# A streaming encoder step on one core: five norms as one product each with a constant matrix, and a first stage loaded by single tiles

## The chip, the core and the metric

The kernel runs on one core of a Trainium2 chip. A core has a matrix engine (TensorE, "PE" in the profile, with its weight loads as "PEld"), a vector engine ("DVE"), a scalar engine ("ACT"), a general engine (GpSimd, "POOL") and a sequencer for transfers (SyncE, "SP"; "SPq" are the transfers that it issues). Each engine works off its own list of instructions in order and waits at semaphores. Matmuls read SBUF and write PSUM. The metric is the device time of one execution in microseconds (us), lower is better; the time of a kernel is the median of several runs.

## What is computed

One layer of a streaming encoder over 320 columns of tokens (256 of a prompt, 64 of a running stream), width 2048. The projection feeds an attention part and a gated part; both are normalised, joined and projected, and a squared-ReLU MLP follows.

```python
def rmsnorm(x, g):
    y = x * lax.rsqrt(jnp.mean(x * x, axis=-1, keepdims=True) + EPS)
    return y * g

z = rmsnorm(x, ln_g) @ w_in                      # 2048 -> 1024 q, 128 k, 128 v, 2048 gated
q, k = rmsnorm(q, q_g), rmsnorm(k, k_g)          # per head of 64
attn = sink_attention(q, k, v, bias, sinks)      # windows of 64-column chunks, 16 heads, 2 kv heads
u, v = gelu(zs)[..., :1024], rmsnorm(gelu(zs)[..., 1024:], g)
sgu = u * (W_s @ v + b_s)
mix = concat(rmsnorm(attn, g_a), rmsnorm(sgu, g_s))
x = x + mix @ w_out
x = x + square(relu(rmsnorm(x, ln_ffn) @ w_up)) @ w_down
```

The changed norms are those of `x` at the start ("rx" in the kernel), of `k` per head ("rk"), of the attention's output ("rm0", after the change "rm_a"), of the gated part's output ("rm1", "rm_s") and of `x` before the MLP ("r2").

## The kernel before

**Layout.** Activations lie transposed: a tile holds 128 rows of a feature dimension and 320 columns of tokens. `xT` has 16 such row tiles. A norm's factor is one number for each token, so it is needed as a 128x320 tile in which every row is the same; it is multiplied in behind the matmuls, when PSUM is read.

**Products.** `products` (L106) works through a weight matrix in chunks of four row tiles by 256 columns. For each chunk it loads `w_raw` (512 KB) on SP's queue; ACT rounds it to `w_hi` (L125), DVE takes the rest `w_lo` (L126), three buffers of each; PE then does `w_hi` times the high part, `w_hi` times the low part and `w_lo` times the high part of the activations (L136), 24 matmuls of 320 columns in a chunk, 96 in a product over 16 row tiles. All products accumulate in two PSUM buffers named `acc`, so that a third one begins only when DVE has read the first.

**First stage.** The first call (L196) makes two products at once: k and v (`kv_ps`, an `acc` buffer) and the first 256 columns of q (`q0_ps`). It also loads `xT` and splits it into `XH` (ACT, L178) and `XL` (DVE, L179). The first four row tiles are loaded one by one and converted in the written order (`keep_in_program_order`), the other twelve in chunks of four.

**The relative bias.** PE makes the bias row (L224), DVE copies it to `b_row` (L226), POOL's queue writes it to device memory as `b_dram` (L228), and 16 transfers of 48 KB read it back into `bias` (L236). These wait in the list `between`, and `load` (L94) puts four of them behind each of the next four weight loads, on the same SP queue. That queue is worked off in order, and the first of them waits until `b_dram` has landed; the weight load that stands behind four bias transfers is issued after them. So the second chunk of the product that follows the first stage (q's second 256 columns, "q1" below) is loaded only when the bias row has made its way.

**Norms.** The squares of `x` are summed on ACT and DVE (`ssq`), those of later norms by `add_square` (L377, ACT and POOL). `rstd_rows` (L154) multiplies the sums by a column of 1/n (three matmuls with one output column, in f32, which the trace shows as six), adds eps on DVE and takes the power -1/2 on POOL: the factors then lie on 128 partitions by 3. `spread` (L165) brings them back along the tokens with three matmuls against the identity, again six in the trace, and a DVE copy. For k (two heads) the same is done with `hsel`, `rkx` and L283.

**Order.** The tile framework's scheduler sets each engine's order from its own timeline, except where `issue_after` or `keep_in_program_order` bind it. x's squares are bound behind step 9 of the first stage (L242), and so is the bias product (L223). What follows q1 in PE's list are the products for q's columns 512 to 1024, four for the gated v with the attention between them, four for u, sixteen of 48 matmuls for `w_out`, and the MLP's 64 products.

Of the kernel before, what the change touches and what calls it, by code (L numbers as in the profile page):

```python
# [29 lines left out]
def hymba_step_kernel(ctx: ExitStack, tc: tile.TileContext, i, o):  # L30
# [55 lines left out]
    hsel = const.tile([P, 2], F32, name="hsel")  # L86
    nc.vector.memset(hsel, 0.0)
    nc.vector.memset(hsel[0:HD, 0:1], 1.0 / HD)
    nc.vector.memset(hsel[HD:P, 1:2], 1.0 / HD)
# [11 lines left out]
    def chunks(n, first):  # L101
        if first:
            return [(a, 1) for a in range(4)] + [(a, 4) for a in range(4, n, 4)]
        return [(a, 4) for a in range(0, n, 4)]

    def products(w, k0, nk, jobs, rh, rl, first=None, deep=None):  # L106
# [4 lines left out]
        for a, n in chunks(nk, first is not None):  # L111
# [4 lines left out]
            for j, (c0, ps) in enumerate(jobs):  # L116
# [7 lines left out]
                pin = tc.keep_in_program_order if first is not None and a < 4 else lambda ins: ins  # L124
# [29 lines left out]
    def rstd_rows(sq, weight, eps, h=1):  # L154

        st = misc()
        for t in range(3):
            nc.tensor.matmul(out=st[:, t * h:t * h + h], lhsT=sq[:, t * P:(t + 1) * P], rhs=weight, start=True, stop=True)  # L158
        r = sm.tile([P, 3 * h], F32, name="r_rows", tag="r_rows")
        nc.vector.tensor_scalar(out=r, in0=st[:, 0:3 * h], scalar1=eps, scalar2=None, op0=ALU.add)  # L160
        rs = sm.tile([P, 3 * h], F32, name="rs_rows", tag="rs_rows")
        nc.gpsimd.tensor_tensor(out=rs, in0=r, in1=nhalf[:, 0:3 * h], op=ALU.pow)
        return rs

    def spread(rs, name):  # L165

        bc = misc()
        for t, (t0, n) in enumerate(TT):
            nc.tensor.matmul(out=bc[:, t0:t0 + n], lhsT=rs[:, t:t + 1].to_broadcast([P, P]),  # L169
                             rhs=ident[:, 0:n], start=True, stop=True)  # L170
        out = sm.tile([P, T], F32, name=name, tag="rstd_b", bufs=2)
        nc.vector.tensor_copy(out=out, in_=bc[:, 0:T])
        return out

# [48 lines left out]
    with tc.issue_after(steps[9][2]):  # L223
        nc.tensor.matmul(out=b_ps[0:16, 0:255], lhsT=tab, rhs=oneh, start=True, stop=True)  # L224
# [27 lines left out]
    zk = sm.tile([P, T], F32, name="zk", tag="w2", bufs=4)
    nc.vector.tensor_tensor(out=zk, in0=kv_ps[:, 0, 0:T], in1=rx, op=ALU.mult)
    nc.vector.tensor_tensor(out=vT, in0=kv_ps[:, 1, 0:T], in1=rx, op=ALU.mult)
    sq = sums("ksq")
    nc.scalar.activation(out=sq[:, 0:T], in_=zk, func=AF.Square)
    rk = rstd_rows(sq, hsel, EPS, 2)
# [3 lines left out]
    def queries(g, q_ps):  # L261
# [8 lines left out]
        for b in range(5):  # L270
# [10 lines left out]
    bc = misc()  # L281
    for t, (t0, n) in enumerate(TT):
        nc.tensor.matmul(out=bc[:, t0:t0 + n], lhsT=rkx[:, t], rhs=ident[:, 0:n], start=True, stop=True)  # L283
    for dst, c in ((kn[:, 0:256], slice(0, 256)), (kn[:, 384:448], slice(256, 320))):
        nc.vector.scalar_tensor_tensor(out=dst, in0=zk[:, c], scalar=g_k, in1=bc[:, c], op0=ALU.mult, op1=ALU.mult)
# [17 lines left out]
    for g in range(1, 4):  # L303
        queries(g, product(w_in, 0, KT, g * 256, xh, xl))
# [98 lines left out]
    acc_v = sums("acc_v")  # L403
# [32 lines left out]
    for g in range(4):  # L436
# [24 lines left out]
    for half, (hi, lo, acc) in enumerate(((AH, AL, acc_a), (SH, SL, acc_s))):  # L461
        rm = spread(rstd_rows(acc, inv_1k, EPS), f"rm{half}")
        for g in range(8):
# [9 lines left out]
    r2 = spread(rstd_rows(acc_x, inv_dm, EPS), "r2")  # L473
# [94 lines left out]
```

## Time and profile before

| | |
|---|---|
| median of 3 runs | 1260.79 us (1259.16 to 1262.47) |
| the profiled execution: device time / span of the instructions | 1262.67 us / 1260.9 us |
| instructions in the trace | 20260 |
| DVE busy | 635.5 us (50% of the span) |
| ACT busy | 488.9 us (39%) |
| POOL busy | 104.1 us (8%) |
| moved by DMA | 187.79 MB, 149 GB/s in the mean |
| mean granted TensorE clock | 0.997 |

The page of a profile gives for each engine the time in which it had an instruction at work. The prediction takes its durations from this one execution. Its device time is 1.8 us over its span (what lies before the first and behind the last instruction), and 1.9 us over the median of the runs.

### The profile page before, as it was taken

How to read it: one execution, taken by the hardware profiler on the slowest of the kernel's cores; microseconds unless marked ns; L12 is line 12 of the kernel's file. 1: busy time of each engine (PE TensorE's matmuls, PEld its weight loads, DVE VectorE, ACT ScalarE, POOL GpSimd, SP SyncE). 2: the span in 40 equal slices, each digit the busy share in tenths (PEclk: the TensorE clock that was granted, in tenths of full speed). 3: DMA queues.
4: the chain of work that ended last, by engine and by line, in shares of the span. 5: the costliest groups of instructions: out<-in, count | busy, mean ns of one | idle time of the engine just before them, and what ended most of it. 6: DMA issues, size and time to landing. Idle time of an engine off the chain costs nothing.

```text
span 1260.9 us, 20260 instructions
## 1 busy us (share of the span) xinstructions
PE 1251.8 (99%) x8559; PEld 1238.0 (98%) x8559; DVE 635.5 (50%) x731; ACT 488.9 (39%) x636; POOL 104.1 (8%) x100
## 2 busy tenths in 40 slices
PE   8999999999999999999999999999999999999998
PEld 7998899999999999999999999999999999999998
DVE  6547857756864444444444444344444334444443
ACT  7335546523543342233333333344333333343221
POOL 1213443400310000000000000000000000000000
PEclk8999999999999999999999999999999999999999
DMA  9553334644445544445544444555444444544550
GB/s 281 168 141 106 97 115 125 213 142 147 148 143 150 151 149 150 150 149 151 151 150 151 151 150 151 151 150 150 151 150 150 145 149 149 150 152 160 170 168 32
DMA packets 186427, 187.79 MB, mean 149 GB/s; under 512 B 6464, under 2 KB 185856, under 8 KB 186336
## 3 DMA queue, kind: packets, MB, share of 16 engines
q1 hardware_dynamic: 185696, 185.43, 47.5%
q0 software_dynamic: 496, 1.03, 0.4%
q8 instruction: 67, 1.10, 0.4%
q14 instruction: 24, 0.20, 0.0%
q10 hardware_dynamic: 144, 0.03, 0.0%
HBM read 182.91 MB, written 3.32 MB: 148 GB/s over the span
## 4 chain that ended last, share of the span: by engine, by line
PE 98%; DMA 1%; SPq 0%; ACT 0%; POOL 0%; issue 0%; DVE 0%; POOLq 0%
PE acc L136 93%; PE misc L136 1%; PE q_ps L136 1%; DMA xT<-in_xT 1%; PE misc L365 1%; PE misc L371 1%; PE s_ps L327 1%; SPq L99 0%; PE misc L271 0%; PE misc L427 0%; PE misc L158 0%; POOL s L355 0%; PE misc L419 0%; PE misc L169 0%; PE misc L428 0%
## 5 line engine op out<-in xcount | busy, mean ns | idle before, releaser
L126 DVE TENSOR_TENSOR w_lo<-w_raw,w_hi 128x1024 fp32r<-128x1024 f32 x332 | 413.0, 1244 | 458.8 <-ACT w_hi L125 449.8
L125 ACT ACTIVATE w_hi<-w_raw 128x1024 fp32r<-128x1024 f32 x332 | 351.8, 1060 | 714.2 <-PE acc L136 675.7
L136 PE MATMUL acc<-H2H,w_hi 128*128 128x320 f32 x1024 | 316.6, 309 | 0.0
L136 PE MATMUL acc<-H2L,w_hi 128*128 128x320 f32 x1024 | 316.4, 309 | 0.0
L136 PE MATMUL acc<-H2H,w_lo 128*128 128x320 f32 x1024 | 316.4, 309 | 0.0
L136 PE MATMUL acc<-FH,w_hi 128*128 128x320 f32 x992 | 306.5, 309 | 0.0
L136 PE MATMUL acc<-FL,w_hi 128*128 128x320 f32 x992 | 306.5, 309 | 0.0
L136 PE MATMUL acc<-FH,w_lo 128*128 128x320 f32 x992 | 306.5, 309 | 0.0
L136 PEld LDWEIGHTS acc<-H2L,w_hi 128*128 128x128 f32 x1024 | 192.2, 188 | 0.0
L136 PEld LDWEIGHTS acc<-H2H,w_hi 128*128 128x128 f32 x1024 | 192.2, 188 | 0.0
L136 PEld LDWEIGHTS acc<-H2H,w_lo 128*128 128x128 f32 x1024 | 192.2, 188 | 0.0
L136 PEld LDWEIGHTS acc<-FH,w_hi 128*128 128x128 f32 x992 | 186.2, 188 | 0.0
L136 PEld LDWEIGHTS acc<-FL,w_hi 128*128 128x128 f32 x992 | 186.2, 188 | 0.0
L136 PEld LDWEIGHTS acc<-FH,w_lo 128*128 128x128 f32 x992 | 186.2, 188 | 0.0
L136 PE MATMUL acc<-XH,w_hi 128*128 128x320 f32 x384 | 117.8, 318 | 0.3 <-ACT w_hi L125 0.3
L136 PE MATMUL acc<-XL,w_hi 128*128 128x320 f32 x384 | 116.9, 316 | 0.0
L136 PE MATMUL acc<-XH,w_lo 128*128 128x320 f32 x384 | 115.7, 312 | 0.0
L136 PEld LDWEIGHTS acc<-XH,w_hi 128*128 128x128 f32 x384 | 71.9, 191 | 4.2 <-issue 2.1
L136 PEld LDWEIGHTS acc<-XL,w_hi 128*128 128x128 f32 x384 | 72.1, 191 | 1.4 <-issue 1.2
L136 PEld LDWEIGHTS acc<-XH,w_lo 128*128 128x128 f32 x384 | 71.1, 188 | 1.3 <-issue 1.2
L485 DVE SCALAR_TENSOR_TENSOR tf<-acc,r 128x640 f32<-128x640 f32 x32 | 26.4, 825 | 42.7 <-PE acc L136 42.7
L499 DVE TENSOR_TENSOR xT<-xT,acc 128x640 f32<-128x640 f32 x31 | 25.5, 821 | 41.8 <-PE acc L136 41.8
(174 smaller groups left out, 1009.5 us busy)
## 6 DMA issues: line engine op xcount, KB each, us to landing
w_raw<-in_w_up SPq DMA_DIRECT2D x128, 512.0 KB
w_raw<-in_w_down SPq DMA_DIRECT2D x128, 512.0 KB
w_raw<-in_w_in SPq DMA_DIRECT2D x44, 512.0 KB
w_raw<-in_w_out SPq DMA_DIRECT2D x32, 512.0 KB
w_first<-in_w_in SPq DMA_DIRECT2D x6, 512.0 KB
out_yT<-xT SPq DMA_DIRECT2D x7, 320.0 KB
xT<-in_xT SPq DMA_DIRECT2D x3, 640.0 KB
w_first<-in_w_in SPq DMA_DIRECT2D x8, 128.0 KB
```

The source lines that it names most:

```text
L125: high = pin(nc.scalar.activation(out=hi[:, :n], in_=raw[:, :n], func=AF.Copy))
L126: low = pin(nc.vector.tensor_tensor(out=lo[:, :n], in0=raw[:, :n], in1=hi[:, :n].bitcast(F32), op=ALU.subtract))
L136: mm = nc.tensor.matmul(out=out, lhsT=w_[:, k, g * P:(g + 1) * P], rhs=r_(kk), start=(kk == 0 and x == 0), stop=(kk == nk - 1 and x == 2))
L327: nc.tensor.matmul(out=s_ps[:, p, j * nk:(j + 1) * nk], lhsT=qT[hs, blk_, a:a + 2].rearrange("p a t -> p (a t)"), rhs=kz[hs, kv, k0:k0 + n ...
L365: nc.tensor.transpose(out=pt_ps[0:n, (2 * p + j) * P:(2 * p + j + 1) * P], in_=s[:, p, j, c:c + n], identity=ident)
L371: nc.tensor.matmul(out=o_ps[p * HD:(p + 1) * HD, 0:256], lhsT=v[0:n, kv], rhs=pt[0:n, p * 256:(p + 1) * 256], start=(x == 0), stop=(x == l ...
L485: nc.vector.scalar_tensor_tensor(out=t, in0=ps[:, :, 0:T], scalar=0.0, in1=r2[:, None, :].to_broadcast([P, 2, T]), op0=ALU.max, op1=ALU.mult)
L499: nc.vector.tensor_tensor(out=xT[:, a:a + n], in0=xT[:, a:a + n], in1=p, op=ALU.add)
```

## The change

1. **`rstd` takes the place of `rstd_rows` and `spread` for five norms** (rx, rk, rm_a, rm_s, r2). The sums are split into a high and a low part (ACT, DVE), and two matmuls of 320 columns with a constant 128x128 matrix (`mean_dm`, `mean_1k`, and `mean_hd` in blocks of 64 for k) give the mean on every partition at once. The power -1/2 is then worked out on DVE over 128x320: eps is added, a first guess is taken from the number's bits, and three Newton steps of three instructions follow, eleven DVE instructions in all. v's norm (`rv`) keeps `rstd_rows`.
2. **The first stage goes by single tiles** for eight row tiles, then two pairs, then one chunk of four; the conversions of the first twelve are kept in the written order.
3. **x's norm stands behind weights**: q1's product is written ahead of it, and rx, k's norm and q's first group are bound behind conversions of q1's chunks. x's squares are bound behind later steps of the first stage.
4. **The bias product** is bound behind step 19 in place of step 9; with the new chunks that is the last matmul of row tiles 10 and 11, where it was the last of row tiles 4 to 7.
5. **The attention's squares** are taken in the first three of the four u products, and rm_a in the fourth; rm_s stands behind the third product of `w_out`.

```diff
+    mean_dm = const.tile([P, P], F32R, name="mean_dm")
+    nc.gpsimd.memset(mean_dm.bitcast(F32), 1.0 / DM)
...
     def chunks(n, first):
         if first:
-            return [(a, 1) for a in range(4)] + [(a, 4) for a in range(4, n, 4)]
+            return [(a, 1) for a in range(8)] + [(8, 2), (10, 2), (12, 4)]
...
-                pin = tc.keep_in_program_order if first is not None and a < 4 else lambda ins: ins
+                pin = tc.keep_in_program_order if first is not None and a < 12 else lambda ins: ins
...
-    def spread(rs, name):
-
-        bc = misc()
-        for t, (t0, n) in enumerate(TT):
-            nc.tensor.matmul(out=bc[:, t0:t0 + n], lhsT=rs[:, t:t + 1].to_broadcast([P, P]),
-                             rhs=ident[:, 0:n], start=True, stop=True)
-        out = sm.tile([P, T], F32, name=name, tag="rstd_b", bufs=2)
-        nc.vector.tensor_copy(out=out, in_=bc[:, 0:T])
+    def rstd(acc, mean, eps, out):
+        hl = sm.tile([P, 2, T], F32R, name="n_hl", tag="w2", bufs=4)
+        hi, lo = hl[:, 0], hl[:, 1]
+        nc.scalar.activation(out=hi, in_=acc, func=AF.Copy)
+        nc.vector.tensor_tensor(out=lo, in0=acc, in1=hi.bitcast(F32), op=ALU.subtract)
+        ps = misc()
+        nc.tensor.matmul(out=ps[:, 0:T], lhsT=mean, rhs=hi, start=True, stop=False)
+        nc.tensor.matmul(out=ps[:, 0:T], lhsT=mean, rhs=lo, start=False, stop=True)
+        xt = sm.tile([P, 2, T], F32, name="n_xt", tag="w2", bufs=4)
+        x, t = xt[:, 0], xt[:, 1]
+        nc.vector.tensor_scalar(out=x, in0=ps[:, 0:T], scalar1=eps, scalar2=3e38, op0=ALU.add, op1=ALU.min)
+        nc.vector.tensor_scalar(out=out.bitcast(I32), in0=x.bitcast(I32), scalar1=-0.5, scalar2=float(0x5F3759DF),
+                                op0=ALU.mult, op1=ALU.add)
+        for _ in range(3):
+            nc.vector.tensor_tensor(out=t, in0=out, in1=out, op=ALU.mult)
+            nc.vector.scalar_tensor_tensor(out=t, in0=t, scalar=-0.5, in1=x, op0=ALU.mult, op1=ALU.mult)
+            nc.vector.scalar_tensor_tensor(out=out, in0=t, scalar=1.5, in1=out, op0=ALU.add, op1=ALU.mult)
         return out
...
-            split(xT[:, k], g_mix[:, k:k + 1], XH[:, k], XL[:, k], pinned=a < 4)
+            split(xT[:, k], g_mix[:, k:k + 1], XH[:, k], XL[:, k], pinned=a < 12)
...
-    with tc.issue_after(steps[9][2]):
+    with tc.issue_after(steps[19][2]):
         nc.tensor.matmul(out=b_ps[0:16, 0:255], lhsT=tab, rhs=oneh, start=True, stop=True)
...
-        with tc.issue_after(steps[9][0]):
+        with tc.issue_after(steps[11 + k // 2][0]):
             nc.scalar.activation(out=sq, in_=xT[:, k:k + 2], func=AF.Square)
...
-    rx = spread(rstd_rows(ssq, inv_dm, EPS), "rx")
+    q1_ps = product(w_in, 0, KT, 256, xh, xl)
+    behind = list(steps)
...
+    with after(0):
+        rx = rstd(ssq, mean_dm, EPS, rstd_b("rx"))
+    with after(1):
+        zk = sm.tile([P, T], F32, name="zk", tag="w2", bufs=4)
...
+        rk = rstd(sq, mean_hd, EPS, rstd_b("rk"))
...
-    queries(0, q0_ps)
-    nc.scalar.activation(out=rkx.rearrange("p t (h d) -> p (t h) d", h=2), in_=rk[:, :, None].to_broadcast([P, 6, HD]),
-                         func=AF.Copy)
...
+    with after(1):
+        queries(0, q0_ps)
...
             with tc.issue_after(high), tc.issue_after(low):
-                add_square(acc_a, ao[:, a], a == 0)
                 split(ao[:, a], g_oa[:, a:a + 1], AH[:, a], AL[:, a])
+        for x, a in enumerate(range(3 * g, min(3 * g + 3, 8))):
+            with tc.issue_after(steps[x][0]):
+                add_square(acc_a, ao[:, a], a == 0)
+        if g == 3:
+            with tc.issue_after(steps[0][0]), tc.issue_after(steps[0][1]):
+                rm_a = rstd(acc_a, mean_1k, EPS, rstd_b("rm_a"))
...
-        rm = spread(rstd_rows(acc, inv_1k, EPS), f"rm{half}")
...
+            if half == 0 and g == 2:
+                rstd(acc_s, mean_1k, EPS, rm_s)
...
-    r2 = spread(rstd_rows(acc_x, inv_dm, EPS), "r2")
+    r2 = rstd(acc_x, mean_dm, EPS, rstd_b("r2"))
```

How the built programs stand at three places follows; a row is an instruction's line, operation, output<-inputs and size, and the numbers behind names tell buffers apart.

PE's list around the bias product, before (L224; `w_hi_261` and `w_lo_262` are row tiles 4 to 7 of q's first columns, `300` to `330` row tiles 8 to 11):

```order
L136 MATMUL q0_ps_120<-XL_116,w_hi_261 128x320 x5
L136 MATMUL q0_ps_120<-XH_115,w_lo_262 128x320 x8
L224 MATMUL misc_437<-oneh_84,tab_83 16x255
L136 MATMUL acc_119<-XH_115,w_hi_300 128x320 x8
L136 MATMUL acc_119<-XL_116,w_hi_300 128x320 x8
L136 MATMUL acc_119<-XH_115,w_lo_301 128x320 x8
```

The same place now (L238; `387` and `388` are row tiles 10 and 11 of q's first columns, `414`, `415`, `443` and `444` row tiles 12 to 15, `517` q1's first chunk):

```order
L140 MATMUL q0_ps_122<-XH_117,w_hi_387 128x320 x4
L140 MATMUL q0_ps_122<-XL_118,w_hi_387 128x320 x4
L140 MATMUL acc_121<-XH_117,w_hi_414 128x320 x8
L140 MATMUL acc_121<-XL_118,w_hi_414 128x320 x8
L140 MATMUL q0_ps_122<-XH_117,w_lo_388 128x320 x4
L238 MATMUL misc_483<-oneh_84,tab_83 16x255
L140 MATMUL q0_ps_122<-XH_117,w_hi_443 128x320 x8
L140 MATMUL q0_ps_122<-XL_118,w_hi_443 128x320 x3
L140 MATMUL acc_121<-XH_117,w_lo_415 128x320 x8
L140 MATMUL q0_ps_122<-XL_118,w_hi_443 128x320 x5
L140 MATMUL q0_ps_122<-XH_117,w_lo_444 128x320 x8
L140 MATMUL acc_515<-XH_117,w_hi_517 128x320
```

The bias product moved from half of the first stage, 96 of its 192 matmuls ahead of it, to 32 matmuls before its end.

DVE's list around the copy of the bias row, before (`w_lo_301` and `w_lo_330` are row tiles 8 to 11, `w_lo_545` q1's first chunk):

```order
L126 TENSOR_TENSOR w_lo_301<-w_first_299,w_hi_300 128x1024
L245 TENSOR_TENSOR ssq2_444<-ssq2_444,sq2_455 128x640
L226 COPY b_row_439<-misc_437 16x255
L126 TENSOR_TENSOR w_lo_330<-w_first_299,w_hi_329 128x1024
L245 TENSOR_TENSOR ssq2_444<-ssq2_444,sq2_458 128x640
```

The same now, with x's norm behind it (`w_lo_518` is q1's first chunk, `w_lo_552` its second, `n_hl` to `rx` the new norm):

```order
L130 TENSOR_TENSOR w_lo_444<-w_first_413,w_hi_443 128x1024
L261 TENSOR_TENSOR ssq_513<-ssq2_490 128x320
L130 TENSOR_TENSOR w_lo_518<-w_raw_516,w_hi_517 128x1024
L240 COPY b_row_485<-misc_483 16x255
L172 TENSOR_TENSOR n_hl_653<-ssq_513,n_hl_653 128x320
L178 TENSOR_SCALAR n_xt_659<-misc_656 128x320
L179 TENSOR_SCALAR rx_652<-n_xt_659 128x320
L182 TENSOR_TENSOR n_xt_659<-rx_652 128x320
L183 SCALAR_TENSOR_TENSOR n_xt_659<-n_xt_659 128x320
L184 SCALAR_TENSOR_TENSOR rx_652<-n_xt_659,rx_652 128x320
L130 TENSOR_TENSOR w_lo_552<-w_raw_550,w_hi_551 128x1024
```

The copy now stands behind the conversion of q1's first chunk, and the second chunk's conversion behind the first instructions of x's norm. On SP's list the part that follows is as it was: q1's first load, four bias transfers, q1's second load, four bias transfers, and so on.

ACT's list in the first stage where single tiles end, before (`200` and `211` are row tile 3 of the two products, `232` row tiles 4 to 7, the XH between them row tile 4):

```order
L178 ACTIVATE XH_115<-xT_81,cols_82 128x320
L125 ACTIVATE w_hi_200<-w_first_124 128x256
L178 ACTIVATE XH_115<-xT_81,cols_82 128x320
L125 ACTIVATE w_hi_211<-w_first_124 128x256
L178 ACTIVATE XH_115<-xT_81,cols_82 128x320 x3
L125 ACTIVATE w_hi_232<-w_first_231 128x1024
```

The place where pairs end now (`370` and `387` are row tiles 10 and 11 of the two products, the four XH row tiles 12 to 15, `414`, `443` and `517` as above):

```order
L193 ACTIVATE XH_117<-xT_81,cols_82 128x320 x2
L129 ACTIVATE w_hi_370<-w_first_330 128x512
L193 ACTIVATE XH_117<-xT_81,cols_82 128x320 x4
L257 ACTIVATE sq2_507<-xT_81 128x640
L257 ACTIVATE sq2_510<-xT_81 128x640
L129 ACTIVATE w_hi_387<-w_first_330 128x512
L129 ACTIVATE w_hi_414<-w_first_413 128x1024
L129 ACTIVATE w_hi_443<-w_first_413 128x1024
L129 ACTIVATE w_hi_517<-w_raw_516 128x1024
```

Before, one weight conversion of row tile 3 stood behind an XH of the next chunk; now one of row tiles 10 and 11 does, behind four XH and two squares.

More of the change, by code (lines that the diff above doesn't have):

```diff
@@ L10 @@
 F32R = mybir.dt.float32r
+I32 = mybir.dt.int32
 AF = mybir.ActivationFunctionType
@@ L140, in sums @@
     def sums(name):
-        t = sm.tile([P, TP], F32, name=name, tag="ssq", bufs=2)
-        nc.gpsimd.memset(t[:, T:TP], 0.0)
-        return t
+        return sm.tile([P, T], F32, name=name, tag="ssq", bufs=2)
     def acc_tile():
@@ L152, in product, with rstd_rows @@
         return ps
-    def rstd_rows(sq, weight, eps, h=1):
+    def rstd_rows(sq, weight, eps):
         st = misc()
         for t in range(3):
[L158 to L162, printed above, removed]
-        return rs
@@ L165, in spread @@
-    def spread(rs, name):
-        bc = misc()
-        for t, (t0, n) in enumerate(TT):
-            nc.tensor.matmul(out=bc[:, t0:t0 + n], lhsT=rs[:, t:t + 1].to_broadcast([P, P]),
-                             rhs=ident[:, 0:n], start=True, stop=True)
-        out = sm.tile([P, T], F32, name=name, tag="rstd_b", bufs=2)
-        nc.vector.tensor_copy(out=out, in_=bc[:, 0:T])
-        return out
+            nc.tensor.matmul(out=st[:, t:t + 1], lhsT=sq[:, t * P:(t + 1) * P], rhs=weight, start=True, stop=True)
@@ new lines, in rstd_rows @@
+        r = sm.tile([P, 3], F32, name="r_rows", tag="r_rows")
+        nc.vector.tensor_scalar(out=r, in0=st[:, 0:3], scalar1=eps, scalar2=None, op0=ALU.add)
+        rs = sm.tile([P, 3], F32, name="rs_rows", tag="rs_rows")
+        nc.gpsimd.tensor_tensor(out=rs, in0=r, in1=nhalf[:, 0:3], op=ALU.pow)
+        return rs
+    def rstd(acc, mean, eps, out):
[15 more added lines that the diff above has]
+            nc.vector.scalar_tensor_tensor(out=out, in0=t, scalar=1.5, in1=out, op0=ALU.add, op1=ALU.mult)
+        return out
@@ L175, in split, with rstd_b @@
+    def rstd_b(name):
+        return sm.tile([P, T], F32, name=name, tag="rstd_b", bufs=2)
     def split(src, g, hi, lo, pinned=False):
@@ L246, in hymba_step_kernel, with after @@
     ssq = sums("ssq")
-    nc.vector.tensor_tensor(out=ssq[:, 0:T], in0=ssq2[:, 0], in1=ssq2[:, 1], op=ALU.add)
-    rx = spread(rstd_rows(ssq, inv_dm, EPS), "rx")
[L252 to L257, printed above, removed]
+    nc.vector.tensor_tensor(out=ssq, in0=ssq2[:, 0], in1=ssq2[:, 1], op=ALU.add)
+    q1_ps = product(w_in, 0, KT, 256, xh, xl)
+    behind = list(steps)
+    def after(n):
+        stack = ExitStack()
+        for ins in behind[n][:2]:
+            stack.enter_context(tc.issue_after(ins))
+        return stack
+    with after(0):
+        rx = rstd(ssq, mean_dm, EPS, rstd_b("rx"))
+    with after(1):
+        zk = sm.tile([P, T], F32, name="zk", tag="w2", bufs=4)
+        nc.vector.tensor_tensor(out=zk, in0=kv_ps[:, 0, 0:T], in1=rx, op=ALU.mult)
+        nc.vector.tensor_tensor(out=vT, in0=kv_ps[:, 1, 0:T], in1=rx, op=ALU.mult)
+        sq = sums("ksq")
+        nc.scalar.activation(out=sq, in_=zk, func=AF.Square)
+        rk = rstd(sq, mean_hd, EPS, rstd_b("rk"))
     rq = at.tile([P, 4, 10], F32, name="rq", bufs=1)
@@ L275, in queries @@
         nc.gpsimd.tensor_tensor(out=rq[:, g], in0=r, in1=nhalf[:, 0:10], op=ALU.pow)
[L277 to L283 removed]
+    with after(1):
+        queries(0, q0_ps)
     for dst, c in ((kn[:, 0:256], slice(0, 256)), (kn[:, 384:448], slice(256, 320))):
[L285 removed]
+        nc.vector.scalar_tensor_tensor(out=dst, in0=zk[:, c], scalar=g_k, in1=rk[:, c], op0=ALU.mult, op1=ALU.mult)
     for h in range(2):
@@ L402, in hymba_step_kernel @@
     gv = blk("gv", [P, 8, T])
-    acc_v = sums("acc_v")
+    acc_v = at.tile([P, TP], F32, name="acc_v", bufs=1)
+    nc.gpsimd.memset(acc_v[:, T:TP], 0.0)
     for g in range(4):
@@ L460, in hymba_step_kernel @@
     acc_x = sums("acc_x")
-    for half, (hi, lo, acc) in enumerate(((AH, AL, acc_a), (SH, SL, acc_s))):
-        rm = spread(rstd_rows(acc, inv_1k, EPS), f"rm{half}")
+    rm_s = rstd_b("rm_s")
+    for half, (hi, lo, rm) in enumerate(((AH, AL, rm_a), (SH, SL, rm_s))):
         for g in range(8):
```

19 lines of the change are left out of this document (9 added, 10 removed).

## The prediction, made before the changed kernel ran

> **What bounds the kernel now.** I read the page's busy times first, then PE's waits, then windows over the beginning, then the chain of waits and the timelines of each engine there. In the page, the matmul engine is at work nearly all the time, and the slices show no hole but at the ends:
>
> ```profile
> PE 1251.8 (99%) x8559; PEld 1238.0 (98%) x8559; DVE 635.5 (50%) x731; ACT 488.9 (39%) x636; POOL 104.1 (8%) x100
> PEclk8999999999999999999999999999999999999999
> ```
>
> PE's waits name all that PE lost to another engine:
>
> ```profile
> PE q_ps L136 <- ACT w_hi L125: 4.0, 2, 3.3
> PE misc L77 <- DVE hsel L87: 1.3, 1, 1.3
> PE acc L136 <- ACT w_hi L125: 0.3, 1, 0.3
> ```
>
> So there is little to win: 4.3 us of waits in the first stage, matmuls that are not the products', and what a slow clock costs. The windows over the first stage (columns: time, busy us of PE, PEld, DVE, ACT and POOL with their counts, granted clock, DMA share, GB/s) show the clock:
>
> ```profile
> 2.50:8.50 6.00, 5.34 (x28) 4.19 (x27) 3.08 (x8) 3.68 (x10) 2.78 (x9) 1.00 0.95 264
> 11.10:14.90 3.80, 0.47 (x5) 0.21 (x3) 0.34 (x1) 0.94 (x3) 0.00 (x0) 0.94 1.04 358
> 14.90:21.40 6.50, 6.16 (x22) 5.76 (x23) 6.06 (x10) 6.50 (x11) 0.00 (x0) 0.51 1.09 357
> 21.40:28.00 6.60, 6.60 (x44) 5.98 (x43) 5.35 (x9) 6.60 (x13) 0.38 (x1) 1.00 1.03 350
> ```
>
> The 3.3 us stall is followed by 6.5 us at a granted clock of 0.51. That costs another 3.2 us.
>
> The chain of waits gives the price of a matmul in a dense stretch, 48.75 / 332 = 0.147 us, and of the small groups:
>
> ```profile
> 241.22 0.56 PE misc L158 x6
> 241.78 6.26 PE acc L136 x42
> 248.05 0.61 PE misc L169 x6
> 248.66 48.75 PE acc L136 x332
> 53.71 1.01 PE misc L271 x10
> 58.49 0.61 PE misc L283 x6
> ```
>
> The 42 matmuls between two groups take 6.26 where 42 x 0.147 is 6.17: each group costs about 0.1 more than its own time.
>
> **The change: the norms on PE.** rm_a, rm_s and r2 each lose an L158 and an L169 group, 0.56 + 0.61 + 0.2 = 1.37 us, and gain two matmuls of 320 columns, 0.29 us. No row shows a product with a constant matrix; the nearest, L136, has the same size, so I take 0.147 each, and the six passes of L169 (0.61 the group) as the upper bound. Gain: 3 x 1.08 = **3.2 us**, between 2.6 and 3.2. POOL's powers and DVE's copy go too; both lay beside matmuls. v's norm stays. rx and rk are counted in the beginning, below.
>
> **The first stage alone.** With single tiles ACT's list no longer holds back row tile 3's weights. Before, they stood behind an XH whose 640 KB load landed late (the first row is from the chain, the others from the timelines: start, duration, engine, line, output<-inputs, and in brackets the idle time before and its releaser):
>
> ```profile
> 6.45 7.49 DMA xT<-in_xT
> 13.96 0.56 ACT L178 ACTIVATE XH<-xT,cols 128x320 fp32r<-128x320 f32 x1 [4.33 <-DMA xT<-in_xT]
> 14.88 0.90 PE L136 MATMUL q_ps<-XH,w_hi 128*128 128x320 f32 x2 [3.33 <-ACT w_hi L125]
> 40.98 0.31 PE L136 MATMUL acc<-XH,w_hi 128*128 128x320 f32 x1
> 58.04 0.31 PE L136 MATMUL acc<-XH,w_lo 128*128 128x320 f32 x1
> ```
>
> The stage's 192 matmuls need 28.2 us; it began at 4.2 and q1 at 40.98 (its last matmul at 58.04). Of the 36.8 us some 8 are lost. The order moves the fault rather than removing it: row tiles 10 and 11's second conversion now stands behind four XH and two squares that need the 640 KB of row tiles 12 to 15. Up to there stand 12 x 0.43 + 0.66 = 5.8 MB; at the windows' 264 GB/s for single tiles and some 356 for the rest they have passed by 20.5 to 22 us, and I put their landing at 22.7. Four XH, two squares and the conversion take 3.7 us more, to 26.4. PE, 132 matmuls in, wants it at 24.2. I take a stall of 2.2 us, and q1 could begin at 36, 5 us earlier; without the stall at 33.8.
>
> **The bias row takes this back.** This term decides. Before, the way from the bias row to q1's second chunk was (timelines again; the last row is from SP's waits):
>
> ```profile
> 26.91 0.41 DVE L226 COPY b_row<-misc 16x255 f32<-16x255 f32 x1 [1.25 <-PE misc L224]
> 27.62 0.58 POOL L228 DMA_DIRECT2D b_dram<-b_row  x1 [22.20 <-DVE b_row L226]
> 29.37 0.53 POOL L218 MEMSET wsT<- 64x512 f32 x1 [1.17 <-DMA wsT<-in_sgu_wT]
> 31.82 2.60 SPq L99 DMA_DIRECT2D bias<-b_dram  x4
> 34.46 0.44 SPq L99 DMA_DIRECT2D w_raw<-in_w_in  x1
> 38.41 1.06 ACT L125 ACTIVATE w_hi<-w_raw 128x1024 fp32r<-128x1024 f32 x1 [4.38 <-DMA w_raw<-in_w_in]
> 39.50 1.22 DVE L126 TENSOR_TENSOR w_lo<-w_raw,w_hi 128x1024 fp32r<-128x1024 f32 x1 [3.19 <-ACT w_hi L125]
> 42.08 1.06 ACT L125 ACTIVATE w_hi<-w_raw 128x1024 fp32r<-128x1024 f32 x1 [2.62 <-PE misc L158]
> 46.44 1.06 ACT L125 ACTIVATE w_hi<-w_raw 128x1024 fp32r<-128x1024 f32 x1 [3.30 <-DMA w_raw<-in_w_in]
> SPq L99 <- DMA b_dram<-b_row: 8.3, 1, 8.3
> ```
>
> From the copy's start to the second chunk's w_hi are 11.5 us, to the third's at most 15.2, to the fourth's 19.5. SP's last row: its queue stood for 8.3 us at the first bias transfer, with the weights behind it. That was free, since PE wanted the second chunk only at 44.5.
>
> Now the copy stands behind w_lo of q1's first chunk. That chunk's load follows wsT's on SP; wsT landed at 29.37. With single tiles going out at 264 GB/s for four tiles longer (1.7 MB, some 1.6 us at most), I put q1's first landing at 30.5 (29.4 to 32). Then w_hi (1.06) and w_lo (1.22): the copy starts at **32.8**, 5.9 us later than before, whatever PE does. PE's bias product allows it too: 4.7 us before the stage's end at 36, so at 31.4. If the stage ends after 37.5, the bias product sets it instead.
>
> So q1's second chunk has its w_hi at 32.8 + 11.5 + 1.06 = 45.4. PE wants it at 36 + 3.5 (first chunk) + 0.3 (rx's mean) = 39.8. A stall of **5.6 us** takes the place of the old one. DVE's first five instructions of rx run in it, and w_lo follows at 46.6; PE can use two matmuls meanwhile. The old stall of 3.3 us was followed by 6.5 us at half clock, so I take the same: PE runs at 0.29 us a matmul until 51.9 and ends the chunk at 52.5, the third at 56.0, the fourth (w_lo ready at 54.6) at 59.5. With rk's mean, the next product starts at 59.8. In the old trace it started 0.147 after 58.04, at 58.2. Behind that point the change still owes L271's group of q's first columns (1.1 with its restart), which the old order had ahead, and is spared L283's (0.7). Loss: 59.8 + 1.1 - 58.2 - 0.7 = **2.0 us**. At full clock the four chunks end at 57.8 and the loss is 0.3. A copy at 31.6 or 35 shifts this by -1.2 or +2.2; the bounds for the clock are 0 and the 3.2 us of the old window.
>
> The Trainium skill, "TensorE: Matmul & The Clock Gate", section "What's actually happening", has the clock fall to half after an idle window of about 3.4 us and rise after a busy one of the same length. This trace agrees on the fall (a wait of 3.33 us) and shows 6.5 us rather than 3.4 for the rise; by the page's window alone the loss at half clock would be an estimated 1.7 us in place of 3.2.
>
> **Beside other work.** DVE gets 12 instructions of 128x320 for each norm; by the nearest row, the copy of rm (0.48), that is 5.8 us, and 0.40 apart where one needn't wait for the other. The one place where this is close: the third product of `w_out` needs the buffer of the first, which is read only when rm_a is done.
>
> ```profile
> 239.79 0.82 DVE L394 TENSOR_TENSOR z<-acc,rx 128x640 f32<-128x640 f32 x1 [0.82 <-PE acc L136]
> 240.74 1.23 DVE L126 TENSOR_TENSOR w_lo<-w_raw,w_hi 128x1024 fp32r<-128x1024 f32 x1
> 241.88 0.52 DVE L397 TENSOR_SCALAR gc<-gc 128x640 f32<-128x640 f32 x1
> 249.63 0.48 DVE L172 COPY rm<-misc 128x320 f32<-128x320 f32 x1
> 250.03 1.86 DVE L179 SCALAR_TENSOR_TENSOR SL<-gv,cols,SH 128x320 fp32r<-128x320 f32 x2
> 251.81 0.81 DVE L466 TENSOR_TENSOR to<-acc,rm 128x640 f32<-128x640 f32 x1
> ```
>
> From the mean's matmuls PE has two products, 14.1 us, and 0.3. From 0.6 us after the mean's start DVE has, up to and with that reading: eleven of the norm (0.44 apart, 4.8 us), four weight conversions (1.14 apart, 4.6), z and three more of gelu and gate (2.7), two splits (0.9) and the reading (0.8): 14.4 us in all, the time that PE has. Where one must wait for ACT or POOL it is late; I take a stall of **0.2 us**, 0 to 1. The attention's squares are as many as before, on engines at work 39% (ACT) and 8% (POOL) of the span. r2 has 18 us for its chain and rm_s no one behind it.
>
> **Sum.** +2.0 - 3.2 + 0.2 = -1.0 us against the profiled execution (1262.67 with a span of 1260.9, so a span near 1260). That execution lies 1.9 over the median of 1260.79; the median after is 1259.8.
>
> **Rivals.**
> - *The first stage's gain is kept.* For it speaks the stall that goes. q1's second chunk would have to be there by 39.8, so the copy by 39.8 - 12.6 = 27.2, near where it was; the order speaks against. Then q1 loses nothing: 5.0 earlier, five norms at 1.08, less 0.2 for `w_out`: 10.2 us, about 1250.6. Chance 0.15.
> - *rm_a's chain holds PE* at the third product of `w_out`. It decides from 14.4 us on, and costs what lies over it; half clock follows if the stall passes some 3.3 us. With DVE a quarter slower than my rows, 18 us, it is 3.6 - 0.2 + 3.2, about 1266.4. For it: DVE's sum has no slack. Against: it is summed from whole durations, and PE waited for nothing there before. Chance 0.10.
> - *Small loads are slow.* Four more tiles go in pieces of 128 and 160 KB. If these moved at half the 264 GB/s of the window 2.5 to 8.5, the copy would start 6.4 us later and the loss would grow by as much, some 1266. The window speaks against. Chance 0.05. The Trainium skill, "DMA: Bandwidth & Descriptors", section "Bandwidth", gives 138 GB/s for 64 KB and asks for 1 MiB; by 138 the sum would come out, as an estimate, at the same 1266. This trace has 264 for its small ones.
>
> **How the numbers follow.** My forecast has 0.70. Its own range is 1256 (full clock, an early copy) to 1264 (a late copy, a us of stall). The runs before spread by 1.7 to either side, so the range that should hold 8 times in 10 is 1254.5 to 1265. A measurement of this kernel tells apart about 0.3%, 3.8 us, so 1257.0 to 1264.6 is "no change". Of the forecast's 0.70, 0.07 lies below and 0.03 above. Faster: 0.15 + 0.07 = 0.22. Slower: 0.10 + 0.05 + 0.03 = 0.18. Within: 0.60.
>
> **What would show it.** Right: the copy of the bias row near 33 us; a wait of PE for w_hi of q1 of 5 to 6 us near 40 to 45, with SP's queue standing at the bias transfers; a granted clock near 0.5 behind it; the product after q1 starting near 60; rm_a, rm_s and r2 without L169's groups. Wrong: q1 without a hole (first rival), a hole near the third `w_out` product (second), first-stage holes before row tile 8 (third). The forecast as a whole falls if the copy of the bias row starts before 29 us.

## The result, and the profile after

| | before | after |
|---|---|---|
| median, runs side by side | 1260.30 us (1258.80 to 1262.47, 6 runs) | 1265.53 us (1264.49 to 1266.04, 6 runs) |
| the profiled execution: device time / span | 1262.67 / 1260.9 us | 1265.31 / 1263.5 us |
| granted clock of the profiled execution | 0.997 | 0.997 |

After over before is 1.0041, with a 95% interval of 1.0028 to 1.0054. On a second chip it was 1.0036 (1.0023 to 1.0049). The change makes the kernel slower by 5.2 us on the first chip and by 3.9 on the second; the prediction had 1 us faster.

The page's busy times after: PE has 3.5 us less to do and 50 matmuls fewer, DVE 25 us more. That is the part of the change that was meant to pay.

```profile
PE 1248.3 (99%) x8509; PEld 1233.5 (98%) x8509; DVE 660.9 (52%) x786; ACT 492.9 (39%) x648; POOL 99.9 (8%) x95
```

PE's waits after (columns: what waited, what for, us in total, times, the longest) show where it went: 10.2 us behind other engines in the rows of `acc` and `q_ps`, where before had 4.3.

```profile
PE acc L140 <- ACT w_hi L129: 5.2, 2, 4.9
PE q_ps L140 <- ACT w_hi L129: 2.2, 1, 2.2
PE acc L140 <- DVE to L493: 2.2, 1, 2.2
PE acc L140 <- DVE w_lo L130: 0.6, 1, 0.6
```

The first and the last are the hole in q1, the second is the stall in the first stage, the third is the third product of `w_out`. The timelines of the first 62 us (start, duration, engine, line, output<-inputs, in brackets the idle time before and its releaser) show the way of the bias row:

```profile
28.10 0.85 PE L140 MATMUL q_ps<-XH,w_hi 128*128 128x320 f32 x4 [2.18 <-ACT w_hi L129]
33.71 0.41 DVE L240 COPY b_row<-misc 16x255 f32<-16x255 f32 x1
34.41 0.58 POOL L242 DMA_DIRECT2D b_dram<-b_row  x1 [3.95 <-DVE b_row L240]
38.72 2.60 SPq L103 DMA_DIRECT2D bias<-b_dram  x4
41.36 0.44 SPq L103 DMA_DIRECT2D w_raw<-in_w_in  x1
41.24 0.31 PE L174 MATMUL misc<-n_hl,mean_dm 128*128 128x320 f32 x1
41.39 0.31 PE L175 MATMUL misc<-n_hl,mean_dm 128*128 128x320 f32 x1
45.49 1.06 ACT L129 ACTIVATE w_hi<-w_raw 128x1024 fp32r<-128x1024 f32 x1 [12.78 <-DMA w_raw<-in_w_in]
46.60 0.41 PE L140 MATMUL acc<-XH,w_hi 128*128 128x320 f32 x1 [4.89 <-ACT w_hi L129]
61.16 0.31 PE L140 MATMUL acc<-XH,w_hi 128*128 128x320 f32 x1
```

The copy of the bias row is at 33.7, the transfers that need it go out at 38.7, q1's second weights behind them, and ACT stands 12.8 us for these weights. The two matmuls of x's mean (L174, L175) stand between q1's first chunk and the hole. The last row is the first matmul of the product after q1. Windows of 3 us (columns: time, length, PE's busy time and count, granted clock, DMA share, GB/s) show the clock behind the hole:

```profile
41.00:44.00 3.00, 0.70 (x5) 1.00 0.56 149
44.00:47.00 3.00, 0.40 (x2) 0.99 0.81 231
47.00:50.00 3.00, 2.37 (x10) 0.50 0.79 240
50.00:53.00 3.00, 3.00 (x13) 0.50 0.79 217
53.00:56.00 3.00, 3.00 (x20) 0.87 0.88 304
```

PE looks fully busy from 50 on, but does 13 matmuls in 3 us where it does 22 at full clock (29 to 32 us). At `w_out` the timelines of DVE, POOL and PE read:

```profile
243.34 0.49 DVE L178 TENSOR_SCALAR n_xt<-misc 128x320 f32<-128x320 f32 x1 [1.66 <-PE misc L175]
246.65 0.49 DVE L183 SCALAR_TENSOR_TENSOR n_xt<-n_xt 128x320 f32<-128x320 f32 x1
247.17 1.75 DVE L184 SCALAR_TENSOR_TENSOR rm_a<-n_xt,rm_a 128x320 f32<-128x320 f32 x1
252.25 0.48 DVE L184 SCALAR_TENSOR_TENSOR rm_a<-n_xt,rm_a 128x320 f32<-128x320 f32 x1
254.19 2.25 DVE L194 SCALAR_TENSOR_TENSOR SL<-gv,cols,SH 128x320 fp32r<-128x320 f32 x2
258.49 1.55 DVE L493 TENSOR_TENSOR to<-acc,rm_a 128x640 f32<-128x640 f32 x2
246.81 1.76 POOL L419 TENSOR_TENSOR gc<-gc,z 128x640 f32<-128x640 f32 x1 [6.74 <-DVE gc L418]
252.98 3.12 POOL L404 TENSOR_TENSOR acc_s<-acc_s,sq 128x320 f32<-128x320 f32 x2 [4.41 <-ACT sq L403]
259.46 0.38 PE L140 MATMUL acc<-AH,w_hi 128*128 128x320 f32 x1 [2.16 <-DVE to L493]
```

The same instruction L184 takes 0.48 us alone and 1.75 while POOL's L419 runs; two splits that take 0.55 apiece elsewhere take 2.25 together while POOL adds. These two places add 1.27 and about 1.2 us to rm_a's chain (from L178 to the first of the two readings at L493), which is what PE waits for.

### The profile page after: what moved, and what is told of

It reads as the page before. It is cut to its first block, busy times and chain, and to the rows that moved or that the text cites. A ratio compares the mean times of both kernels' runs of the same rounds, so it can differ in the third digit from the quotient of the medians.

```text
span 1263.5 us, 20243 instructions
## 1 busy us (share of the span) xinstructions
PE 1248.3 (99%) x8509; PEld 1233.5 (98%) x8509; DVE 660.9 (52%) x786; ACT 492.9 (39%) x648; POOL 99.9 (8%) x95
## 4 chain that ended last, share of the span: by engine, by line
PE 95%; DMA 2%; DVE 1%; SPq 1%; issue 0%; ACT 0%; ACTq 0%; DVEq 0%
PE acc L140 91%; PE misc L140 1%; DMA w_raw<-in_w_in 1%; SPq L103 1%; PE misc L392 1%; PE s_ps L348 1%; DMA w_first<-in_w_in 1%; PE misc L386 1%; DVE w_lo L130 1%; DMA b_dram<-b_row 0%; DMA xT<-in_xT 0%; PE misc L296 0%; PE misc L449 0%; PE misc L441 0%; ACT w_hi L129 0%
```

## The experiments

Each group was run beside the kernel before on one chip; "before" is its median there, and a ratio is to that.

**The bias row early, in two ways.** The theory: the hole in q1 comes from the bias row's place alone. `e1_bias_early` puts its product earlier; `e2_bias_behind` leaves it and sends the bias transfers behind q1's weights.

```diff
-    with tc.issue_after(steps[19][2]):
+    with tc.issue_after(steps[11][2]):
```

> The changed kernel, with the bias product bound behind row tile 5 (step 11) in place of row tiles 10 and 11. Theory (the bias row's copy comes late, and SP's queue holds q1's second chunk behind the bias transfers): the copy starts before 20 us, PE's wait of 4.9 us in q1 and the half clock behind it are gone, and the product after q1 starts near 52 us in place of 61, so about 1256.6 us. Rival (the weights land late for another reason, such as the smaller loads): the hole stays and the time is 1265 to 1266.

```diff
+    later = []
...
-                between.append((bias[hh * HD:(hh + 1) * HD, p, j], src))
+                later.append((bias[hh * HD:(hh + 1) * HD, p, j], src))
...
+    between.extend(later)
```

> The changed kernel, with the bias product and its copy left late, but the 16 bias transfers handed to SP's queue only behind q1's four weight loads. Theory (the queue's order is what holds the weights): the hole in q1 goes although the copy stays near 33 us, about 1256.6 us. Rival 1 (PE, DVE or the loads themselves are late): the hole stays, 1265 to 1266. Rival 2 (the hole only moves to the next product, whose weights now stand behind the transfers): less than half is won, 1261 to 1264.

Before was 1262.12. e1: 1267.92, ratio 1.0047 (1.0032 to 1.0061); e2: 1268.28, 1.0049 (1.0032 to 1.0065). Both missed by some 11 us, though the hole did go. PE's longest waits of e1, then the longest of e2:

```profile
PE acc L140 <- ACT ksq L281: 7.7, 1, 7.7
PE q_ps L140 <- ACT w_hi L129: 2.9, 2, 2.6
PE acc L140 <- DVE to L493: 2.2, 1, 2.2
```

```profile
PE acc L140 <- ACT ksq L283: 7.7, 1, 7.7
```

and e1's timelines around q1's end:

```profile
39.23 0.31 PE L174 MATMUL misc<-n_hl,mean_dm 128*128 128x320 f32 x1
53.16 0.31 PE L175 MATMUL misc<-n_hl,mean_dm 128*128 128x320 f32 x1
53.51 0.49 DVE L178 TENSOR_SCALAR n_xt<-misc 128x320 f32<-128x320 f32 x1 [1.50 <-PE misc L175]
59.65 0.49 DVE L184 SCALAR_TENSOR_TENSOR rx<-n_xt,rx 128x320 f32<-128x320 f32 x1
60.18 0.49 DVE L278 TENSOR_TENSOR zk<-acc,rx 128x320 f32<-128x320 f32 x1
61.21 0.61 PE L140 MATMUL acc<-XH,w_hi 128*128 128x320 f32 x1 [7.74 <-ACT ksq L281]
```

The two matmuls of x's mean stand 14 us apart: the second is now the last thing of q1 in PE's list. rx is worked out only behind it; the product after q1 needs the `acc` buffer of k and v, which `zk` reads with rx. So a new hole of 7.7 us opens at q1's end, where PE has nothing else. In the changed kernel both matmuls stood behind q1's first chunk (41.24 and 41.39). The edit touches only the bias product, so it was the scheduler that moved the second one; in e2 it moved both, to 51.1 and 51.2 at q1's end. So e1 and e2 traded one hole for another, and do not show what the changed kernel's own order would do without the hole of the bias row. `e5_norm_ahead`, below, fixes the place of the means as well.

**Fewer adds on POOL.** The kernel leaves out the last group's squares in `acc_s` (two squares on ACT and two adds on POOL), so one norm's sums are short.

```diff
-            add_square(acc_s, gv[:, a], a == 0)
+            if g < 3:
+                add_square(acc_s, gv[:, a], a == 0)
```

> The changed kernel without the last group's two squares and their POOL additions in the gated part's norm, which leaves two of its eight row tiles out of the sum. Theory (POOL's work at the same time stretches DVE's two splits from 0.55 to 1.16 us and one Newton step from 0.49 to 1.75): the two splits take 0.55 each, and PE's wait for rm_a's reading before the third product of w_out shrinks from 2.2 to about 1.0 us. Rival (the chain of eleven is too long in itself): the wait stays at 2.2 us.

One run, 1263.03. The waits and DVE's timeline:

```profile
PE acc L140 <- DVE to L494: 0.9, 1, 0.9
```

```profile
246.16 1.75 DVE L184 SCALAR_TENSOR_TENSOR rm_a<-n_xt,rm_a 128x320 f32<-128x320 f32 x1
253.19 1.00 DVE L194 SCALAR_TENSOR_TENSOR SL<-gv,cols,SH 128x320 fp32r<-128x320 f32 x2
```

The edit changes POOL's adds and ACT's squares together. Without them the two splits take 1.00 in place of 2.25, and the wait falls from 2.2 to 0.9. L184 still meets POOL's L419 and still takes 1.75. So POOL's adds lengthen the splits beside them, and the splits lengthen the wait by as much. That L419 does the same to L184 rests on the rows alone; it was not taken away.

**The bias row late in the kernel before.** `e4_before_bias_late` is the kernel before with one edit:

```diff
-    with tc.issue_after(steps[9][2]):
+    with tc.issue_after(steps[11][2]):
```

> The kernel before with one edit: the bias product bound behind row tiles 8 to 11 (step 11) in place of 4 to 7. Theory: the copy starts some 7.5 us later, near 34.5 us, q1's second chunk is ready near 47.1 where PE wants it at 45.2, and the time grows by about 2 us, to 1262.3. Rival (the queue's order does not matter there): no change, 1260.3 us.

1266.19 against 1262.12, ratio 1.0033 (1.0020 to 1.0046): +4.1 us where 2 were expected. Its waits:

```profile
PE acc L136 <- ACT w_hi L125: 2.9, 2, 1.7
PE acc L136 <- DVE w_lo L126: 0.6, 1, 0.6
```

The hole is there, with none of the change's other edits: SP's queue stands 14.8 us at the first bias transfer (8.3 before), and q1's second load goes out behind it at 40.89. The size was missed because half clock follows the hole (granted clock 0.78 from 44 to 50 us, 0.65 from 50 to 56, a loss of 0.22 x 6 + 0.35 x 6 = 3.4 us), which the expectation had left out. In the profile the product after q1 begins at 63.84, against 58.19 before.

**Both faults mended, then the third, then the fourth.** `e5_norm_ahead` is e1 with x's norm written ahead of q1's product; `e6_rma_earlier` is e5 with attention's mean one u product earlier; `e7_all_pinned` is e6 with every conversion of the first stage in the written order.

```diff
+    rx = rstd(ssq, mean_dm, EPS, rstd_b("rx"))
     q1_ps = product(w_in, 0, KT, 256, xh, xl)
...
-    with after(0):
-        rx = rstd(ssq, mean_dm, EPS, rstd_b("rx"))
```

> The changed kernel with two edits: the bias product is issued in the first stage (as in e1) and x's norm is written ahead of q1's product, so that its two small products stand at q1's start. Theory (the 4.8 us hole of q1 and the 7.7 us at q1's end are one conflict: bias row late, or norm late): neither hole is left, q1 runs through at full clock, the next product starts near 52 us instead of 61.3; the wait of 2.2 us ahead of the third w_out product stays. Against the kernel before about -5.6 (stage) -3.2 (norms) +2.2 (w_out) = -6.6 us, ratio about 0.995. Rival (rx's chain on VectorE is too long among q1's conversions, so a hole opens anyway): a wait of 3 us or more for zk or a w_hi, and a time within 0.2% of before or above it.

```diff
-        for x, a in enumerate(range(3 * g, min(3 * g + 3, 8))):
+        for x, a in enumerate(range(4 * g, min(4 * g + 4, 8))):
...
-        if g == 3:
+        if g == 2:
```

> e5 with the four squares that rm_a's mean needs pulled forward into the first two u products and the mean one product earlier. Theory (the third w_out product waits because rm_a's chain on VectorE, stretched by GpSimd's work, ends 2.2 us too late): the wait is gone or under 0.5 us, 2.2 us less than e5. Rival (squares and adds pulled forward lengthen the VectorE queue ahead of the split instead, or PE waits for the squares at the mean): no change, or a wait of the same size elsewhere.

```diff
-                pin = tc.keep_in_program_order if first is not None and a < 12 else lambda ins: ins
+                pin = tc.keep_in_program_order if first is not None and a < 16 else lambda ins: ins
...
-            split(xT[:, k], g_mix[:, k:k + 1], XH[:, k], XL[:, k], pinned=a < 12)
+            split(xT[:, k], g_mix[:, k:k + 1], XH[:, k], XL[:, k], pinned=a < 16)
```

> e6 with every conversion of the first stage pinned to the engine order of its first tiles, so that q1's w_hi no longer stands behind the squares that wait for x's last row tiles. Theory (that wait in the first stage costs 2.2 to 2.6 us plus what it does to the clock): q1 starts some 2 us earlier, 2 to 4 us less than e6, so about 11 us under the kernel before, ratio about 0.991. Rival (the last row tiles' arrival bounds the stage whatever the order is): same as e6 within 0.1%.

> The kernel with all four edits (bias product early, x's norm ahead of q1's weights, attention's mean one product earlier, all first conversions in written order) once more, with more rounds. If the four terms add up (norms -3.2, first stage and its clock -5, no new wait): 1.5 to 3 us below what the same kernel without the last edit gave (1254.9, ratio 0.9946), ratio 0.992 to 0.994 of before, and most executions at a granted clock of 0.999 or 1.0, as the only wait left in the first 300 us is about 1 us. Rival (the last edit moves nothing that counts): ratio 0.9946 again, clocks between 0.997 and 1.0 as without it.

| | median | ratio | before there |
|---|---|---|---|
| e5_norm_ahead | 1258.61 (10 runs) | 0.9980 (0.9968 to 0.9992) | 1261.66 |
| e6_rma_earlier | 1254.87 (4 runs) | 0.9946 (0.9928 to 0.9965) | 1261.66 |
| e7_all_pinned | 1254.08 (4 runs) | 0.9946 (0.9927 to 0.9965) | 1261.66 |
| e7_again | 1253.59 (6 runs) | 0.9943 (0.9931 to 0.9956) | 1260.79 |

In e5 the x-norm's means ran at 37.9 and 38.8, q1 had no hole, and the next product started where it was expected, near 52:

```profile
52.28 0.31 PE L140 MATMUL acc<-XH,w_hi 128*128 128x320 f32 x1
```

The time fell by 3.1 us and not by 6.6. Its runs go from 1256.29 at a granted clock of 1.0 to 1261.77 at 0.996, so the runs with half clock took up to 5.5 us longer. But that alone is not the shortfall: at a granted clock of 1.0 the two runs of e5 took 1256.29 and 1256.70, the three of before beside them 1259.32 to 1259.77, which is 3.1 us again. The 5.6 us expected of the stage seem to go by the profile of before, where the product after q1 began at 58.19 and half clock is in it. e6 removed the wait at `w_out` and 3.7 us by the medians. The last edit, of e7, is within the noise: beside e6 it gave 0.8 us by the medians where 2 to 4 were expected and the same ratio, and e7_again's ratio of 0.9943 lies above the 0.992 to 0.994 expected. In e7_again's trace two squares still stand ahead of the conversion of row tiles 10 and 11 and wait for the load of row tiles 12 to 15, so a stall of 1.4 us is left. Whether the edit changes the clock is open: in e6 and in e7_all_pinned two of four runs are at 1.0, in e7_again, on another chip, five of six. PE's waits in e7_again are down to

```profile
PE q_ps L140 <- ACT w_hi L129: 1.4, 1, 1.4
PE misc L78 <- DVE hone L91: 1.3, 1, 1.3
```

This version beats both kernels, by 7.2 us the one before.

**The terms one by one.** `f1_late_norms` is the kernel before with `rstd` for rm_a, rm_s and r2 alone and attention's mean early enough that nothing waits; `f2_rma_alone` is the changed kernel with e6's edit alone; `after_again` is the changed kernel on the same chip. f1's edit, beside the new `rstd`:

```diff
-                add_square(acc_a, ao[:, a], a == 0)
                 split(ao[:, a], g_oa[:, a:a + 1], AH[:, a], AL[:, a])
+        for x, a in enumerate(range(4 * g, min(4 * g + 4, 8))):
+            with tc.issue_after(steps[x][0]):
+                add_square(acc_a, ao[:, a], a == 0)
+        if g == 2:
+            with tc.issue_after(steps[0][0]), tc.issue_after(steps[0][1]):
+                rm_a = rstd(acc_a[:, 0:T], mean_1k, EPS, rstd_b("rm_a"))
...
-        rm = spread(rstd_rows(acc, inv_1k, EPS), f"rm{half}")
...
+            if half == 0 and g == 2:
+                rstd(acc_s[:, 0:T], mean_1k, EPS, rm_s)
...
-    r2 = spread(rstd_rows(acc_x, inv_dm, EPS), "r2")
+    r2 = rstd(acc_x[:, 0:T], mean_dm, EPS, rstd_b("r2"))
```

> The kernel before with three of its norms alone (attention's, the gated stage's and the second one of x) made as the change makes them, with attention's mean one u product earlier than the change has it, so that nothing waits; the first stage, the bias row and the first norms stay as before. Theory (the prediction's first term, 3 x 1.08 us of products off TensorE): 3.2 us less than before, ratio 0.9975, the waits of the first 60 us as before, no wait ahead of w_out. Rival (the norms' products were partly hidden, or their work on VectorE delays what follows): less than 1 us, ratio above 0.999, or a new wait of 1 us or more behind 190 us.

> The changed kernel with attention's mean one u product earlier (four squares in each of the first two) and nothing else. Theory (2.2 us of the loss is the third w_out product waiting for VectorE): 2.2 us less than the changed kernel on the same chip, 3 to 4 us less where the wait brought half clock with it, and the wait of 4.8 us in q1 stays. Rival (the wait had slack behind it): the same time as the changed kernel.

> The changed kernel beside the two others on one chip: 1.0041 of before (1.0028 to 1.0054) again, with runs at a granted clock of 0.997 or less, as its wait of 4.8 us in q1 lets the clock fall in every execution. If some of its runs show 0.999 or 1.0 and are 3 us shorter, half clock is a matter of chance there too.

Before was 1261.27 (19 runs). f1: 1259.10, ratio 0.9979 (0.9969 to 0.9989). f2: 1262.24, 1.0010 (1.0001 to 1.0019). The changed kernel again: 1265.16, 1.0036 (1.0023 to 1.0049). PE's busy time in f1 against before's 1251.8:

```profile
PE 1248.6 (99%) x8529; PEld 1234.9 (98%) x8529; DVE 651.8 (52%) x761; ACT 490.5 (39%) x639; POOL 104.0 (8%) x99
```

3.2 us of work are gone, as expected; the medians give 2.2, with the interval (1.4 to 3.9 us) around both. In f2 the wait for `to` is gone and q1's hole stays:

```profile
PE acc L140 <- ACT w_hi L129: 4.9, 2, 4.6
PE q_ps L140 <- ACT w_hi L129: 2.3, 1, 2.3
```

So by medians on one chip the loss of 3.9 us is -2.2 (late norms) +3.1 (first stage, f2 less f1) +2.9 (`w_out`, changed kernel less f2).

**Before, once more.** `before_again` profiles the kernel before a second time.

> The kernel before, profiled a second time. If the 2.4 us between the profiled execution of before (1262.67) and its median (1260.3) is a window of half clock that some executions have and others not, a second profile has its half-clock window in the first 60 us shorter, longer or elsewhere while the waits are the same to 0.2 us. If the waits differ, it is arrival of transfers.

One run, 1262.50, span 1260.7 against 1260.9. The waits differ (2.9 and 1.1 us in the first stage, where it was 4.0 and 0.3), which the expectation had set as the sign of the arrival of transfers. Half clock differs too: it is shorter behind the stall (granted clock 0.74 from 14.9 to 21.4 us in place of 0.51), but PE does only 23 matmuls from 2.5 to 8.5 us in place of 28, and q1 begins at 40.86 against 40.98. So this second profile does not show an execution without half clock, and does not tell the two causes apart. The runs' own clocks go with the time: of the 11 runs of before beside e7_again, the five at a granted clock of 1.0 took 1259.29 to 1260.32, the five at 0.997 or 0.998 took 1261.30 to 1263.50. All 11 runs of the changed kernel, on both chips, lie at 0.995 to 0.997.

## Why the prediction was wrong, step by step

A landmark common to all kernels is v's norm, the six small matmuls on `acc_v`. In the kernels made from the changed one it stands seven product matmuls later in PE's list (7195 behind it, against 7202), 1.0 us, which the second column takes off.

| profiled | v's norm starts | against 188.5 | from there to the span's end |
|---|---|---|---|
| before | 188.5 | 0 | 1072.4 |
| before_again | 188.4 | -0.1 | 1072.3 |
| f1_late_norms | 188.0 | -0.5 | 1069.3 |
| after | 192.7 | +3.2 | 1070.8 |
| after_again | 190.6 | +1.1 | 1072.3 |
| f2_rma_alone | 192.9 | +3.4 | 1068.4 |
| e3_no_adds | 191.7 | +2.2 | 1069.6 |
| e5_norm_ahead | 184.4 | -5.1 | 1072.3 |
| e7_again | 183.3 | -6.2 | 1068.4 |

- **The norms on PE (-3.2).** Right: f1 is 3.1 shorter behind the landmark and 3.2 in PE's busy time; f2 and e7_again, 4.0 shorter with the 1.0 of the landmark, show 3.0. The lower bound of 2.6 does not follow from the 0.61 that the step names (3 x 0.76 = 2.3), but nothing hangs on it.
- **The stall in the first stage (2.2 us, behind the squares that wait for row tiles 12 to 15).** Right in place; that the size came out as well (2.18 us at 28.10) is luck. Both ends of the wait came 1.7 us later than forecast, and in after_again, the same kernel, it is 0.9 us, because ACT has row tiles 12 to 15 at 23.10 there and at 24.34 here (22.7 was forecast). q1 began at 37.73, in after_again at 36.48, and not at 36.
- **"The bias row takes this back" (+2.0).** The mechanism was right in each link: copy at 33.7 (forecast 32.8), the second w_hi done at 46.55 (45.4), half clock behind, next product at 61.16 (59.8). The term was somewhat small: each link was 0.9 to 1.4 us late, and it measured +3.2 in the profile and +3.1 by the runs, within the bounds that the step gave for a late copy. The four profiles with this first stage lie on both sides of it (3.2 in after, 1.1 in after_again, 3.4 in f2, 2.2 in e3). The first rival, the first stage's gain kept once the copy is early, is not refuted by e1 and e2, where x's means had moved to q1's end: e5, with the means at q1's start, keeps 5.1 us at the landmark where the rival had 5.0. Its sum of 10.2 us did not come in any kernel; the best, e7, gained 7.2 and 7.6 by the medians.
- **The third product of `w_out` (+0.2).** This step failed by most: 2.2 us of wait in each profile, 2.4 in the span behind the landmark (1070.8 against f2's 1068.4), 3.9 where half clock followed (after_again and e5), 2.9 by the medians. Its place and its rule (14.4 us wanted, 14.4 to be had) were right. The error lies in two terms of the sum. From 0.56 us behind the start of the mean to the end of the reading VectorE took 16.0 us (243.34 to 259.32) where the sum has 13.8 (its 14.4 holds the start as well), and that difference of 2.2 is the wait. The two splits took 2.2 us in place of 0.9; the row quoted above that sentence showed two splits in 1.86, and the sum used less than half of it. The eleven instructions of the norm took 5.9 in place of 4.8, as one of them ran beside POOL's L419; no row that the prediction shows has VectorE beside that instruction. The conversions, gelu and the reading came within 0.1 each. The second rival named this mechanism and gave it one chance in ten. Its condition for half clock, a stall of some 3.3 us, did not hold either (see the last section).
- **"That execution lies 1.9 over the median; the median after is 1259.8".** This step failed too. The terms were worked out against an execution with half clock in its first stage, and the sum was then moved down to a median of executions of which only a part has it. All 11 runs of the changed kernel show a granted clock of 0.997 or less, and each of its profiles has the hole in q1 (4.9 and 4.8 us); of the 11 runs of before beside e7_again five are at 1.0. Against the profiled execution of before the change costs 2.6 us of span; against the median of the runs beside it 5.2, and 3.9 on the other chip.

In sum: -1.0 was forecast; the profile has +3.2 (first stage) -3.0 (norms) +2.4 (`w_out`) = +2.6, which is the difference of the spans, 1263.5 less 1260.9. The rest of the measured 5.2 is the 2.4 by which the profiled execution of before lay above its median, and the 0.2 by which that of after lay below its own. That half clock makes this 2.4 rests on how the runs' times go with their clocks; no execution of before without half clock was profiled.

## What to carry to other kernels

Before a chain is moved behind other work, ask which buffer it holds and what else sets its end: here an edit that took one hole away let the scheduler move x's means to where they opened another, and in the first stage only fixing both places gained anything. So look at the built lists again behind each edit. A row of the trace that shows an instruction at twice its usual time is a term of the sum, not noise to be averaged away; look which other engine ran beside it. And where a kernel has executions with and without a spell of half clock, compare like with like: a profile with half clock and a median of mixed runs differ by as much as a change of this size is worth.

## What the runs showed of the hardware that was not expected

**Half clock comes in pieces of about 3.4 us, and not after every wait.** Five executions waited equally long at the third `w_out` product: 2.15 to 2.16 us in after, e1, after_again, e2 and e5. The clock stayed full in after and e1 and fell in the other three. Windows of 2 us behind the restart, of three of them, first after (restart at 259.46), then after_again (257.35), then e5 (251.09):

```profile
260.00:262.00 2.00, 2.00 (x15) 1.00 0.41 143
```

```profile
258.00:260.00 2.00, 2.00 (x11) 0.60 0.34 120
260.00:262.00 2.00, 2.00 (x9) 0.54 0.48 144
```

```profile
252.00:254.00 2.00, 2.00 (x11) 0.64 0.26 93
254.00:256.00 2.00, 2.00 (x9) 0.50 0.62 189
```

In the first there is none, in the others (0.40 + 0.46) / 0.5 x 2 = 3.4 us and (0.36 + 0.50) / 0.5 x 2 = 3.4 us at half. After the hole of 4.9 us in q1 it was 6.8 us, twice that, and 6.8 in the profile of before (0.06 / 0.5 x 3.8 + 0.49 / 0.5 x 6.5, from the two windows at its stall); around e1's hole of 7.7 us it was 10.3, three times. The Trainium skill, "TensorE: Matmul & The Clock Gate", section "What's actually happening", has a window of 3.4 us that runs freely, so that its effect varies between runs; these rows agree. It has the clock fall after one idle window; here a wait of 2.2 us, shorter than that, was enough in three executions of five. Why some waits bring two pieces, others one or none was not tried.

**VectorE and GpSimd hold each other up.** VectorE's L184 reads two tiles of SBUF; it took 0.48 us alone and 1.75 beside GpSimd's L419, which had begun 0.36 us before it and ended 1.40 after its start: it ran on for some 0.35 us from there, as if it had begun to work only then. The Trainium skill, "SBUF — State Buffer", section "Who interferes with whom", says that a VectorE instruction with two inputs from SBUF contends with a GpSimd instruction that reads SBUF, and that this contention is an exclusive lock. The rows of after and the shorter splits of e3 (1.00 in place of 2.25 us) agree.
